# Head outputs turned on VectorE in 32 x 32 squares, layer-norm rows kept on chip, second-norm transposes moved behind later products: one layer of a hybrid conformer / mLSTM backbone

## Chip, core and metric

The kernel runs on one core of one Trainium2 chip. The metric is the device time of one execution, in microseconds (us). TensorE (PE) does matmuls and transposes, VectorE (DVE) and ScalarE (ACT) work element by element, GpSimd (POOL) does small odd work and issues some DMAs, SyncE (SP) issues nearly all other DMAs. Each engine works through its own list of instructions strictly in that list's order; an instruction whose data or buffer isn't ready holds up all that stand behind it on its engine.

## What is computed

One layer (D = 1024) on 512 latent tokens with a prefix of 256 context tokens, all in float32:

```
h  = modulate(rmsnorm(x))                        # six modulation vectors from silu(c) @ w_mod
p  = h @ w_in                                    # GLU, q, k, v, output gate, mLSTM gates, two branch gates
u  = dwconv31(p0 * sigmoid(p1))
A  = silu(layernorm(u)) @ w_conv_out             # conformer branch
hm = rms(bidirectional mLSTM(q, k, v)) * norm_g * sigmoid(p5)    # 4 heads of 512
B  = hm @ w_mlstm_out
x  = x + gate1 * ((sigmoid(gA) * A + sigmoid(gB) * B) @ w_out)
x  = x + gate2 * (relu(modulate(rmsnorm(x)) @ w1) ** 2 @ w2)
out = rmsnorm(x) * final_g
```

## The kernel before

Every float32 product is done as three matmuls of split operands, high x high, high x low, low x high (`mm3`, one line each, L104 to L106). A weight piece of 128 x 1024 (`wpiece`) is loaded by SP into `wraw` (3 buffers), cast to its high part `whi` on ACT (L99), and its low part `wlo` is made on DVE (L100); `whi` and `wlo` have 4 buffers each, so the cast of a piece has to wait until the matmuls of the piece four earlier are over. PSUM is shared out in two rings of four banks, `bank` and `bank_a`.

A planner sets the order of the instructions on every engine when the kernel is built, from the order in which the code is written, its estimates of durations, and a few explicit bounds (`issue_after`). What stands in the list then is fixed.

The stages that the change touches, in order of time:

1. **Head gates** (`finish`, L300): eight transposes make `pz` in PSUM, a copy on DVE (L305) brings it into `zm`. It is used by all heads; the next projection's matmuls (`p`) take over the PSUM bank.
2. **Heads** (`attend`, L448 to L560): for each of 4 heads and 4 token tiles t, the output `po` (128 tokens x 512) is normed into `hm` on ACT and DVE (L553, L555). `store` then transposes `hm` on PE in four blocks of 128 x 128 (`th`, L541), ACT copies them out scaled by the norm weight (L544) into `st`, and SP stores 256 KB to `hd` in DRAM, in runs of 512 B (L546).
3. **Layer norm of the conformer branch** (`lnfinish`, L397): mean and inverse deviation (`lns`) are written to DRAM (`lnd`) and come back as `lnr`. The branch's 8 tiles `cv` (one buffer named "big") are loaded from DRAM, normed on DVE (L665, L666), put through SiLU on ACT (L667) and split into `act` (L109, L110).
4. **Gate pieces and conformer output**: the last four branch-gate products `pab` (i = 12 to 15) each hold one of the four `bank` buffers until ACT has taken their sigmoid (L678, `sig12` to `sig15`). The conformer output products `pc`, with the pieces of `wco`, follow on PE and need `act`, the first `wco` piece, and a free bank, hence `sig12`. `hmload` reads the heads' output back (`hraw`), and splits it into `hmT`, whose space is that of earlier tiles.
5. **Modulation dots** (`mod`, L654): 32 dots of 128 x 1024 on DVE with rows `wmt` that POOL loads, spread between weight pieces; the last eight make the second gate vector, which goes through `row` (a transpose `pr` and a trip through DRAM) to the row `ga2`.
6. **Output product and second norm** (L785 to L816): for each of 4 token tiles, the last part of `pwo`, the residual `x`, two squares with sums (L799), the factor, two scaled halves `xh` (L808, L810), two groups of four transposes `pt` (L813), and the split into `h2T`. The first feed-forward products (`ff1(0)`, `pf`) run over the first 256 tokens, then over the second 256.

Of the kernel before, what the change touches and what calls it, by code (L numbers as in the profile page):

```python
# [47 lines left out]
def block(ctx, tc, a, out):  # L48
# [22 lines left out]
    zm = cst.tile([P, 8, 64], F32, name="zm")  # L71

# [15 lines left out]
    wlast = [None]  # L88

# [13 lines left out]
    def mm3(dst, l, r, start, stop):  # L103
        mm(dst, lhsT=l[0], rhs=r[0], start=start, stop=False)  # L104
        mm(dst, lhsT=l[0], rhs=r[1], start=False, stop=False)  # L105
        mm(dst, lhsT=l[1], rhs=r[0], start=False, stop=stop)  # L106

    def split(hi, lo, src):
        nc.scalar.copy(out=hi, in_=src)  # L109
        nc.vector.tensor_tensor(out=lo, in0=src, in1=hi.bitcast(F32), op=ALU.subtract)  # L110
# [25 lines left out]
    lnd = dr.tile([2, P, T], F32, name="lnd")  # L136
# [8 lines left out]
    with ExitStack() as hs:  # L145
# [108 lines left out]
        def gates():  # L254
            with tc.tile_pool(name="p1", bufs=1) as p1:
# [44 lines left out]
                def finish():  # L300
                    pz = bank("pz")
                    for i in range(8):
                        nc.tensor.transpose(pz[:, i * 64:(i + 1) * 64], Z[:, i // 4, (i % 4) * P:(i % 4 + 1) * P],
                                            ident[0:64, 0:64])
                    nc.vector.tensor_copy(out=zm.rearrange("p a b -> p (a b)"), in_=pz)  # L305
# [74 lines left out]
        ln = {n: hqa.tile([P, T], F32, name=f"ln{n}") for n in ("m0", "s1", "s2")}  # L380
# [16 lines left out]
        def lnfinish():  # L397
            mu, rv = ln["s1"], ln["s2"]
            p1_, p2_ = bank("ps1"), bank("ps2")
            mm(p1_, lhsT=ones, rhs=ln["s1"], start=True, stop=True)  # L400
            mm(p2_, lhsT=ones, rhs=ln["s2"], start=True, stop=True)
            nc.scalar.activation(out=mu, in_=p1_, func=AF.Copy, scale=1.0 / D)
            sq = hq2.tile([P, T], F32, tag="cacc", name="sq")
            nc.scalar.activation(out=sq, in_=mu, func=AF.Square)
            nc.vector.scalar_tensor_tensor(out=rv, in0=p2_, scalar=1.0 / D, in1=sq, op0=ALU.mult, op1=ALU.subtract)
            nc.vector.tensor_scalar(out=rv, in0=rv, scalar1=0.0, scalar2=None, op0=ALU.max)
# [41 lines left out]
        def attend(h, he, he2, khi, klo, qhi, qlo, more, mid):  # L448
# [87 lines left out]
            pend = None  # L536

            def store(t, hm):
                th = bank_a("th")
                for i in range(4):  # L540
                    nc.tensor.transpose(th[:, i * P:(i + 1) * P], hm[:, i * P:(i + 1) * P], ident)  # L541
# [4 lines left out]
                nc.sync.dma_start(out=hd[4 * h:4 * h + 4, :, t * P:(t + 1) * P].rearrange("i p t -> p i t"), in_=st)  # L546
            for t in range(NT):
# [15 lines left out]
            return lambda: store(*pend)  # L563
# [20 lines left out]
        for h in range(H):  # L584
            if h:
                kh = k_proj(h)
                last()
                if h == H - 1:
                    glu_tile(7)
                qh = q_proj(h)  # L590
            if h < H - 1:
                last = attend(h, he, he2, *kh, *qh, lambda: glu_steps(2 * h + 1), None)
            else:
                last = attend(h, he, he2, *kh, *qh,
                              lambda: [lambda i=i: ab_early(i) for i in range(NS + NX, NS + NX + NE)], lnend)
            if h < H - 1:
                glu_tile(2 * h + 2)
        last()


    with ExitStack() as fs:
# [47 lines left out]
        def mod():  # L649
# [3 lines left out]
            with tc.issue_after(wlast[0].ins):  # L653
# [10 lines left out]
        for j in range(KT):  # L664
            nc.vector.tensor_tensor(out=cv[j], in0=cv[j], in1=lnr[0], op=ALU.subtract)  # L665
            nc.vector.tensor_tensor(out=cv[j], in0=cv[j], in1=lnr[1], op=ALU.mult)  # L666
            lsilu = nc.scalar.activation(out=cv[j], in_=cv[j], func=AF.Silu, scale=ccol(O_LG + j), bias=ccol(O_LB + j))  # L667
# [24 lines left out]
        def hmload(k):  # L692
# [7 lines left out]
            split(hm_[k][:, 0, :], hm_[k][:, 1, :], raw)  # L700
# [68 lines left out]
        while mraw:  # L769
            mod()  # L770
# [14 lines left out]
        for t in range(NT):  # L785
            tt = slice(t * P, (t + 1) * P)
            sq = m2p.tile([P, 4], F32, tag="ss", name="ss")
            def last_part(n):
                nn = slice(n * 512, (n + 1) * 512)
                for k in range(NP1, KT):  # L790
                    w = ws[k]
                    mm3(po[2 * t + n], (yT[k][:, 0, tt], yT[k][:, 1, tt]), (w[0][:, 0, nn], w[1][:, 0, nn]),
                        False, k == KT - 1)

            def residual(n):
                nn = slice(n * 512, (n + 1) * 512)
                nc.vector.tensor_tensor(out=x1[t][:, nn], in0=po[2 * t + n], in1=x1[t][:, nn], op=ALU.add)
                xh = t2("xh")
                nc.scalar.activation(out=xh, in_=x1[t][:, nn], func=AF.Square, scale=1.0 / 32.0,  # L799
                                     accum_out=sq[:, n:n + 1])  # L800
            for n in range(2):
                last_part(n)
                residual(n)
            rstd2(sq)
            for hf in range(2):
                hh = slice(hf * 512, (hf + 1) * 512)
                xh = t2("xh")
                nc.vector.scalar_tensor_tensor(out=xh, in0=x1[t][:, hh], scalar=sq[:, 3:4], in1=aff2[:, hh],  # L808
                                               op0=ALU.mult, op1=ALU.mult)
                nc.vector.tensor_tensor(out=xh, in0=xh, in1=sh2[:, hh], op=ALU.add)  # L810
                pt = bank_a("pt2")
                for k in range(4):
                    nc.tensor.transpose(pt[:, k * P:(k + 1) * P], xh[:, k * P:(k + 1) * P], ident)  # L813
# [6 lines left out]
        ga2 = row(modc[:, 5, :], m1p.tile([P, D], F32, tag="r2", name="ga2"))  # L820
# [3 lines left out]
        def w1load(g):  # L824
            r = []
            for i in range(4):
                w = wpiece(a["w1"][4 * g + i], (KT, P))
                r.append([[w[p_][:, k, :] for k in range(KT)] for p_ in range(2)])
            return r

        def ff1(g, ws):
# [4 lines left out]
            for o, n in ((0, 256), (256, 256)) if g == 0 else ():  # L836
                for i in range(4):
# [152 lines left out]
```

## Time and profile before

| what | value |
|---|---|
| median of 3 runs | 1356.4 us (1356.16 to 1357.19) |
| the profiled execution, its own time | 1357.05 us |
| its span, first to last instruction | 1355.3 us |
| busy: PE, DVE, ACT, POOL | 1324.4, 936.7, 602.5, 68.9 us |
| mean granted TensorE clock | 0.995 of full |
| HBM read and written | 163.0 and 12.3 MB, 129 GB/s over the span |

The 1.75 us between the profiled execution's time and its span lie outside the instructions. PE works for 98% of the span, so the time is told by the PE's work and by the few places where it stands idle or runs at a lower clock.

### The profile page before, as it was taken

Reading aid. Unit: us, or ns where it says so; the run is one execution under the profiler, and the core shown is the slowest. Engines: PE = TensorE matmul, PEld = TensorE weight load, DVE = VectorE, ACT = ScalarE, POOL = GpSimd, SP = SyncE. Lnnn points to the kernel's source line nnn. Section 1 sums busy time; section 2 is a strip of 40 time slices with the busy share of each in tenths; the row PEclk is TensorE's granted clock in tenths of the full one; section 3 lists DMA queues with packets and bytes.
Section 4 is the critical chain, followed back from the end, with each engine's and each line's share of the span. In section 5 each row is a group of like instructions: output and inputs, shape, how many; then the busy total and the mean of one; then the engine's idle time right before and its main releaser. Section 6 shows DMA issues by size and latency. Waiting matters only on the chain.

```text
span 1355.3 us, 16676 instructions
## 1 busy us (share of the span) xinstructions
PE 1324.4 (98%) x6266; PEld 1104.1 (81%) x6266; DVE 936.7 (69%) x1457; ACT 602.5 (44%) x912; POOL 68.9 (5%) x231
## 2 busy tenths in 40 slices
PE   5999999999999999999999999999999999999997
PEld 3788788888888888888888878888798888888885
DVE  5789978489674896748995477766684454554535
ACT  4548664346533465344635274322354323342223
POOL 2000100000000000000000000100000000000001
PEclk9999999999999999999999999999989999999999
DMA  9793233223332233322334479765633322333202
GB/s 329 288 334 110 89 112 105 62 63 101 104 94 67 64 100 107 96 63 66 106 96 127 124 249 312 262 189 200 219 106 96 97 92 63 123 109 109 73 22 78
DMA packets 65205, 176.36 MB, mean 130 GB/s; under 512 B 6594, under 2 KB 19042, under 8 KB 65124
## 3 DMA queue, kind: packets, MB, share of 16 engines
q1 hardware_dynamic: 60516, 158.51, 36.0%
q0 software_dynamic: 4608, 16.78, 3.9%
q8 instruction: 49, 0.80, 0.2%
q14 instruction: 32, 0.26, 0.1%
HBM read 162.99 MB, written 12.27 MB: 129 GB/s over the span
## 4 chain that ended last, share of the span: by engine, by line
PE 88%; DVE 4%; ACT 2%; DMA 2%; issue 1%; POOL 1%; SPq 0%; POOLq 0%; ACTq 0%; DVEq 0%
PE pf L104 8%; PE pf L105 8%; PE pf L106 8%; PE pv L105 3%; PE pv L104 3%; PE pv L106 3%; PE pym L106 2%; PE pym L105 2%; PE pym L104 2%; PE p L104 2%; PE p L106 2%; PE p L105 2%; PE pq L106 2%; PE pq L104 2%; PE pq L105 2%; PE pg L104 2%
## 5 line engine op out<-in xcount | busy, mean ns | idle before, releaser
L99 ACT CAST whi<-wraw 128x1024 fp32r<-128x1024 f32 (+1 forms) x159 | 164.9, 1040 | 305.7 <-PE pv L106 74.6
L100 DVE TENSOR_TENSOR wlo<-wraw,whi 128x1024 fp32r<-128x1024 f32 (+1 forms) x159 | 191.6, 1206 | 87.9 <-ACT whi L99 87.4
L372 DVE SCALAR_TENSOR_TENSOR ca<-up,col,ca 128x512 f32<-128x512 f32 x240 | 179.5, 748 | 5.7 <-ACT ca L370 0.9
L332 DVE SCALAR_TENSOR_TENSOR cacc<-craw,col,cacc 128x512 f32<-128x512 f32 (+1 forms) x128 | 110.7, 876 | 0.0
L864 ACT CAST w2h<-w2raw 128x1024 fp32r<-128x1024 f32 x32 | 32.3, 1052 | 156.3 <-PE pf L106 124.8
L105 PE MATMUL pf<-w2l,fT 128*128 128x512 f32 x256 | 99.6, 390 | 0.0
L104 PE MATMUL pf<-w2h,fT 128*128 128x512 f32 x256 | 99.2, 390 | 0.2 <-ACT w2h L864 0.2
L106 PE MATMUL pf<-w2h,fT 128*128 128x512 f32 x256 | 99.5, 389 | 0.0
L884 DVE TENSOR_TENSOR x<-pf,x 128x512 f32<-128x512 f32 x64 | 44.0, 689 | 65.8 <-PE pf L106 65.7
L104 PE MATMUL pf<-h2T,whi 128*128 128x512 f32 x224 | 87.1, 389 | 0.0
L105 PE MATMUL pf<-h2T,whi 128*128 128x512 f32 x224 | 87.1, 389 | 0.0
L106 PE MATMUL pf<-h2T,wlo 128*128 128x512 f32 x224 | 87.1, 389 | 0.0
L104 PE MATMUL pv<-whi,hT 128*128 128x512 f32 x192 | 75.4, 393 | 0.0
L106 PE MATMUL pv<-whi,hT 128*128 128x512 f32 x192 | 74.7, 389 | 0.0
L105 PE MATMUL pv<-wlo,hT 128*128 128x512 f32 x192 | 74.7, 389 | 0.0
L862 DVE TENSOR_TENSOR w2raw<-w2raw,ga 128x1024 f32<-128x1024 f32 x32 | 39.2, 1225 | 47.5 <-DMA w2raw<-in_w 46.4
L104 PEld LDWEIGHTS pf<-w2h,fT 128*128 128x128 f32 x256 | 48.0, 188 | 10.7 <-ACT w2h L864 0.7
L105 PEld LDWEIGHTS pf<-w2l,fT 128*128 128x128 f32 x256 | 48.1, 188 | 10.6 <-DVE w2l L869 0.7
L106 PEld LDWEIGHTS pf<-w2h,fT 128*128 128x128 f32 x256 | 48.1, 188 | 9.8
L104 PE MATMUL p<-whi,hT 128*128 128x512 f32 x128 | 50.8, 397 | 2.2 <-DVE zm L305 2.2
L869 DVE TENSOR_TENSOR w2l<-w2raw,w2h 128x512 fp32r<-128x512 f32 x64 | 40.7, 686 | 15.0 <-ACT w2h L864 15.0
L104 PE MATMUL pg<-hT,whi 128*128 128x512 f32 x128 | 50.6, 395 | 0.0
(354 smaller groups left out, 3344.1 us busy)
## 6 DMA issues: line engine op xcount, KB each, us to landing
wm<-in_wmt SPq DMA_DIRECT2D x32, 512.0 KB, 6.0
wmt<-in_wmt POOLq DMA_DIRECT2D x32, 512.0 KB, 4.7
wraw<-in_wqk SPq DMA_DIRECT2D x32, 512.0 KB, 3.5
wraw<-in_w SPq DMA_DIRECT2D x32, 512.0 KB, 4.7
w2raw<-in_w SPq DMA_DIRECT2D x32, 512.0 KB, 3.6
wraw<-in_wglu SPq DMA_DIRECT2D x16, 512.0 KB, 3.8
wraw<-in_wp SPq DMA_DIRECT2D x16, 512.0 KB, 3.6
wraw<-in_wv SPq DMA_DIRECT2D x16, 512.0 KB, 3.5
```

What stands on the lines that cost most here:

```text
L99: nc.scalar.copy(out=hi[:, s], in_=raw[:, s])
L100: wlast[0] = nc.vector.tensor_tensor(out=lo[:, s], in0=raw[:, s], in1=hi[:, s].bitcast(F32), op=ALU.subtract)
L104: mm(dst, lhsT=l[0], rhs=r[0], start=start, stop=False)
L105: mm(dst, lhsT=l[0], rhs=r[1], start=False, stop=False)
L106: mm(dst, lhsT=l[1], rhs=r[0], start=False, stop=stop)
L332: nc.vector.scalar_tensor_tensor(out=acc[:, :n], in0=raw[:, d:d + n], scalar=ccol(wc + d), in1=acc[:, :n], op0=ALU.mult, op1=ALU.add)
L372: nc.vector.scalar_tensor_tensor(out=accv, in0=up[:, :, d:d + 64], scalar=w_, in1=accv, op0=ALU.mult, op1=ALU.add)
L862: nc.vector.tensor_tensor(out=raw, in0=raw, in1=ga2, op=ALU.mult)
L864: nc.scalar.copy(out=hi, in_=raw)
L869: nc.vector.tensor_tensor(out=l_, in0=raw[:, nn], in1=hi[:, nn].bitcast(F32), op=ALU.subtract)
L884: nc.vector.tensor_tensor(out=x1[t][:, nn], in0=pf, in1=x1[t][:, nn], op=ALU.add)
```

## The change

- The heads' `th` transposes and scaled copies are gone. DVE turns `hm` within 32 x 32 squares (one instruction for 128 x 512), and four DMAs for each token tile put the squares in their places in DRAM, in runs of 128 B. The norm weight is multiplied in when `hmload` splits the rows.
- `store` follows its tile at once, no longer one tile later.
- `lns` stay on chip, without the trip to DRAM.
- `zm` is copied by ACT.
- In the second norm, the squares' unused result goes into the PSUM of `pwo`; the transposes of tile 0 are bound behind the last part of tile 2, those of tile 1 behind that of tile 3, those of tiles 2 and 3 behind the first half of `ff1(0)`.
- The dots that are left over at that point come after the splits into `h2T`, and `ga2` is made after `ff1(0)`.

```diff
+    lns = [cst.tile([P, T], F32, name=f"lns{i}") for i in range(2)]
...
-                    nc.vector.tensor_copy(out=zm.rearrange("p a b -> p (a b)"), in_=pz)
+                    nc.scalar.copy(out=zm.rearrange("p a b -> p (a b)"), in_=pz)
...
-        ln = {n: hqa.tile([P, T], F32, name=f"ln{n}") for n in ("m0", "s1", "s2")}
+        ln = {"m0": hqa.tile([P, T], F32, name="lnm0"), "s1": lns[0], "s2": lns[1]}
...
-            nc.sync.dma_start(out=lnd[0], in_=mu)
-            nc.sync.dma_start(out=lnd[1], in_=rv)
...
-            pend = None
             def store(t, hm):
-                th = bank_a("th")
+                st = he.tile([P, HD], F32, tag="st", name="st")
+                nc.vector.transpose(out=st, in_=hm)
                 for i in range(4):
-                    nc.tensor.transpose(th[:, i * P:(i + 1) * P], hm[:, i * P:(i + 1) * P], ident)
-                st = he.tile([P, 4, P], F32, tag="st", name="st")
-                for i in range(4):
-                    nc.scalar.activation(out=st[:, i, :], in_=th[:, i * P:(i + 1) * P], func=AF.Copy,
-                                         scale=ccol(O_MG + 4 * h + i))
-                nc.sync.dma_start(out=hd[4 * h:4 * h + 4, :, t * P:(t + 1) * P].rearrange("i p t -> p i t"), in_=st)
+                    nc.sync.dma_start(
+                        out=hd[4 * h:4 * h + 4, :, t * P + 32 * i:t * P + 32 * i + 32].rearrange(
+                            "k (b r) c -> r (k b) c", r=32),
+                        in_=st[32 * i:32 * i + 32, :].rearrange("r (b c) -> r b c", c=32))
             for t in range(NT):
...
-                if pend:
-                    store(*pend)
-                pend = (t, hm)
+                store(t, hm)
...
-        lnr = []
-        for i in range(2):
-            r_ = t2(f"lnr{i}")
-            nc.sync.dma_start(out=r_, in_=lnd[i])
-            lnr.append(r_)
...
-        def mod():
+        def mod(after=None):
             if not mraw:
                 return
             ch, j, raw = mraw.popleft()
-            with tc.issue_after(wlast[0].ins):
+            with tc.issue_after((after or wlast[0]).ins):
...
-            split(hm_[k][:, 0, :], hm_[k][:, 1, :], raw)
+            nc.scalar.activation(out=hm_[k][:, 0, :], in_=raw, func=AF.Copy, scale=ccol(O_MG + k))
+            nc.vector.scalar_tensor_tensor(out=hm_[k][:, 1, :], in0=raw, scalar=ccol(O_MG + k),
+                                           in1=hm_[k][:, 0, :].bitcast(F32), op0=ALU.mult, op1=ALU.subtract)
...
-        while mraw:
-            mod()
...
+        sqs = [m2p.tile([P, 4], F32, name=f"ss{t}", bufs=1) for t in range(NT)]
+        xhs = {}
+        tlast = [None]
+        def last_part(t):
             tt = slice(t * P, (t + 1) * P)
-            sq = m2p.tile([P, 4], F32, tag="ss", name="ss")
-            def last_part(n):
+            for n in range(2):
                 nn = slice(n * 512, (n + 1) * 512)
                 for k in range(NP1, KT):
                     w = ws[k]
                     mm3(po[2 * t + n], (yT[k][:, 0, tt], yT[k][:, 1, tt]), (w[0][:, 0, nn], w[1][:, 0, nn]),
                         False, k == KT - 1)
-            def residual(n):
-                nn = slice(n * 512, (n + 1) * 512)
                 nc.vector.tensor_tensor(out=x1[t][:, nn], in0=po[2 * t + n], in1=x1[t][:, nn], op=ALU.add)
-                xh = t2("xh")
-                nc.scalar.activation(out=xh, in_=x1[t][:, nn], func=AF.Square, scale=1.0 / 32.0,
-                                     accum_out=sq[:, n:n + 1])
-            for n in range(2):
-                last_part(n)
-                residual(n)
-            rstd2(sq)
+                nc.scalar.activation(out=po[2 * t + n], in_=x1[t][:, nn], func=AF.Square, scale=1.0 / 32.0,
+                                     accum_out=sqs[t][:, n:n + 1])
+            rstd2(sqs[t])
+            return mlast[0]
+        def scaled(t, hf):
+            hh = slice(hf * 512, (hf + 1) * 512)
+            xh = xhs[t, hf] = t2("xh")
+            nc.vector.scalar_tensor_tensor(out=xh, in0=x1[t][:, hh], scalar=sqs[t][:, 3:4], in1=aff2[:, hh],
+                                           op0=ALU.mult, op1=ALU.mult)
+            nc.vector.tensor_tensor(out=xh, in0=xh, in1=sh2[:, hh], op=ALU.add)
+        def turned(t, after):
+            tt = slice(t * P, (t + 1) * P)
             for hf in range(2):
-                hh = slice(hf * 512, (hf + 1) * 512)
-                xh = t2("xh")
-                nc.vector.scalar_tensor_tensor(out=xh, in0=x1[t][:, hh], scalar=sq[:, 3:4], in1=aff2[:, hh],
-                                               op0=ALU.mult, op1=ALU.mult)
-                nc.vector.tensor_tensor(out=xh, in0=xh, in1=sh2[:, hh], op=ALU.add)
                 pt = bank_a("pt2")
-                for k in range(4):
-                    nc.tensor.transpose(pt[:, k * P:(k + 1) * P], xh[:, k * P:(k + 1) * P], ident)
+                with tc.issue_after(after.ins):
+                    for k in range(4):
+                        nc.tensor.transpose(pt[:, k * P:(k + 1) * P], xhs[t, hf][:, k * P:(k + 1) * P], ident)
                 ptv = pt.rearrange("p (k t) -> p k t", k=4)
                 kk = slice(4 * hf, 4 * hf + 4)
-                split(h2T[:, 0, kk, tt], h2T[:, 1, kk, tt], ptv)
+                tlast[0] = split(h2T[:, 0, kk, tt], h2T[:, 1, kk, tt], ptv)
+        last_part(0)
+        scaled(0, 0)
+        scaled(0, 1)
+        last_part(1)
+        scaled(1, 0)
+        turned(0, last_part(2))
+        scaled(1, 1)
+        l3 = last_part(3)
+        scaled(2, 0)
+        turned(1, l3)
+        def rest(after):
+            scaled(2, 1)
+            scaled(3, 0)
+            turned(2, after)
+            scaled(3, 1)
+            turned(3, after)
...
-        ga2 = row(modc[:, 5, :], m1p.tile([P, D], F32, tag="r2", name="ga2"))
...
+                mod(tlast[0])
...
+                if o:
+                    rest(mlast[0])
...
+            if g == 0:
+                ga2 = row(modc[:, 5, :], m1p.tile([P, D], F32, tag="r2", name="ga2"), m_)
```

How the lists of the engines change at the places that the prediction speaks of (rows of one kind in a row are counted, x4; names of the kernel after have other line numbers).

ACT before, from the last SiLUs of `cv` to the sigmoids `sig12` to `sig15` of the four `pab` (named here by their buffers, 6730 to 6733); the `whi` in it is that of the second `wco` piece, that of the first stands ahead of the first SiLU:

```order
L667 ACTIVATE cv<-cv,col 128x512 x2
L109 CAST act<-cv 128x512 x2
L667 ACTIVATE cv<-cv,col 128x512
L109 CAST act<-cv 128x512 x3
L99 CAST whi<-wraw 128x1024
L678 ACT_TABLE_LOAD
L678 ACTIVATE sig_6730<-pab 128x512
L678 ACTIVATE sig_6731<-pab 128x512
L678 ACTIVATE sig_6732<-pab 128x512
L109 CAST hmT<-hraw 128x512
L678 ACTIVATE sig_6733<-pab 128x512
```

The same place on ACT after, from the first two `wco` pieces on; `sig12` to `sig15` are 6643 to 6646:

```order
L101 CAST whi<-wraw 128x1024 x2
L654 ACT_TABLE_LOAD
L654 ACTIVATE cv<-cv,col 128x512 x4
L101 CAST whi<-wraw 128x1024
L654 ACTIVATE cv<-cv,col 128x512 x3
L101 CAST whi<-wraw 128x1024
L654 ACTIVATE cv<-cv,col 128x512
L111 CAST act<-cv 128x512 x8
L687 ACTIVATE hmT<-hraw,col 128x512 x3
L665 ACT_TABLE_LOAD
L665 ACTIVATE sig_6643<-pab 128x512
L665 ACTIVATE sig_6644<-pab 128x512
```

All four `wco` casts, eight splits and three of `hmT` now stand ahead of `sig12`, where two casts and the eight splits stood before.

DVE after, from the third `wco` piece's low part (first row) and the last `hm` turned to the splits of `act` and `hmT`; `lns_82` and `lns_83` are the rows that stay on chip:

```order
L102 TENSOR_TENSOR wlo<-wraw,whi 128x1024
L538 STREAM_TRANSPOSE st<-hm 128x512
L652 TENSOR_TENSOR cv<-cv,lns_82 128x512 x2
L653 TENSOR_TENSOR cv<-cv,lns_83 128x512 x2
L652 TENSOR_TENSOR cv<-cv,lns_82 128x512
L641 SCALAR_TENSOR_TENSOR wmt,modc<-wmt,cB 128x1024
L653 TENSOR_TENSOR cv<-cv,lns_83 128x512
L102 TENSOR_TENSOR wlo<-wraw,whi 128x1024
L641 SCALAR_TENSOR_TENSOR wmt,modc<-wmt,cB 128x1024
L644 TENSOR_TENSOR modc<-modc,col 128x8
L112 TENSOR_TENSOR act<-cv,act 128x512 x8
L688 SCALAR_TENSOR_TENSOR hmT<-hraw,col,hmT 128x512 x8
```

Before, the whole norm of `cv` and the splits `act` stood ahead of the first `wlo` of `wco`; now the first three `wlo`, three dots and two turned tiles stand ahead of and between the passes of the norm, and the fourth `wlo` with a dot ahead of the splits.

ACT after, at the head gates:

```order
L321 COPY craw<-pk 128x256
L101 CAST whi<-wraw 128x1024
L322 COPY craw<-pl 128x512
L306 COPY zm<-pz 128x512
L331 ACTIVATE cacc<-craw,col 128x770
```

The copy `zm` stands right behind the copy of `pl` and ahead of the next convolution step; before, it was on DVE, behind two steps of convolutions (`ca`, `cacc`).

PE after, the second half of the second norm, at the turn between the two halves of `ff1(0)`:

```order
L108 MATMUL pf<-h2T,w1l 128x256
L805 MATMUL pt_8265<-ident,xh 128x128 x4
L805 MATMUL pt_8272<-ident,xh 128x128 x4
L805 MATMUL pt_8282<-ident,xh 128x128 x4
L106 MATMUL pf<-h2T,w1h 128x256 x4
L805 MATMUL pt_8289<-ident,xh 128x128 x4
```

The groups are those of tiles 2 and 3; before, they stood between matmuls of the last parts and of the first half.

More of the change, by code (lines that the diff above doesn't have):

```diff
@@ L88, in block @@
     wlast = [None]
+    mlast = [None]
     def wpiece(src, shape, scale=None):
@@ L105, in mm3 @@
         mm(dst, lhsT=l[0], rhs=r[1], start=False, stop=False)
-        mm(dst, lhsT=l[1], rhs=r[0], start=False, stop=stop)
+        mlast[0] = mm(dst, lhsT=l[1], rhs=r[0], start=False, stop=stop)
     def split(hi, lo, src):
         nc.scalar.copy(out=hi, in_=src)
-        nc.vector.tensor_tensor(out=lo, in0=src, in1=hi.bitcast(F32), op=ALU.subtract)
+        return nc.vector.tensor_tensor(out=lo, in0=src, in1=hi.bitcast(F32), op=ALU.subtract)
     hT = [hp.tile([P, 2, TOK], F32R, tag="h", name=f"hT{k}") for k in range(KT)]
@@ L135, in block @@
     sd = dr.tile([NS + NX + NE, P, T], F32, name="sd")
-    lnd = dr.tile([2, P, T], F32, name="lnd")
     queue = deque()
@@ L562, in attend @@
             pump(9)
-            return lambda: store(*pend)
         glu_tile(0)
@@ L586, in block @@
                 kh = k_proj(h)
-                last()
                 if h == H - 1:
@@ L591, in block @@
             if h < H - 1:
-                last = attend(h, he, he2, *kh, *qh, lambda: glu_steps(2 * h + 1), None)
+                attend(h, he, he2, *kh, *qh, lambda: glu_steps(2 * h + 1), None)
             else:
-                last = attend(h, he, he2, *kh, *qh,
+                attend(h, he, he2, *kh, *qh,
                               lambda: [lambda i=i: ab_early(i) for i in range(NS + NX, NS + NX + NE)], lnend)
@@ L597, in block @@
                 glu_tile(2 * h + 2)
-        last()
     with ExitStack() as fs:
@@ L664, in block @@
         for j in range(KT):
-            nc.vector.tensor_tensor(out=cv[j], in0=cv[j], in1=lnr[0], op=ALU.subtract)
-            nc.vector.tensor_tensor(out=cv[j], in0=cv[j], in1=lnr[1], op=ALU.mult)
+            nc.vector.tensor_tensor(out=cv[j], in0=cv[j], in1=lns[0], op=ALU.subtract)
+            nc.vector.tensor_tensor(out=cv[j], in0=cv[j], in1=lns[1], op=ALU.mult)
             lsilu = nc.scalar.activation(out=cv[j], in_=cv[j], func=AF.Silu, scale=ccol(O_LG + j), bias=ccol(O_LB + j))
@@ L699, in hmload, with row @@
             nc.sync.dma_start(out=raw, in_=hd[k])
-            split(hm_[k][:, 0, :], hm_[k][:, 1, :], raw)
+            nc.scalar.activation(out=hm_[k][:, 0, :], in_=raw, func=AF.Copy, scale=ccol(O_MG + k))
+            nc.vector.scalar_tensor_tensor(out=hm_[k][:, 1, :], in0=raw, scalar=ccol(O_MG + k),
+                                           in1=hm_[k][:, 0, :].bitcast(F32), op0=ALU.mult, op1=ALU.subtract)
         for k in range(16):
             queue.append(lambda k=k: hmload(k))
-        def row(src, r_):
+        def row(src, r_, after=None):
             pr = bank("pr")
-            nc.tensor.transpose(pr[0:KT, 0:P], src, ident)
+            with tc.issue_after((after or mlast[0]).ins):
+                nc.tensor.transpose(pr[0:KT, 0:P], src, ident)
             t_ = t2("rowt", P)
@@ L784, in block @@
         h2T = big([P, 2, KT, T], F32R, "h2T")
-        for t in range(NT):
+        sqs = [m2p.tile([P, 4], F32, name=f"ss{t}", bufs=1) for t in range(NT)]
+        xhs = {}
+        tlast = [None]
+        def last_part(t):
             tt = slice(t * P, (t + 1) * P)
-            sq = m2p.tile([P, 4], F32, tag="ss", name="ss")
-            def last_part(n):
+            for n in range(2):
                 nn = slice(n * 512, (n + 1) * 512)
@@ L903, in block @@
             ft = ff1(g, w1)
+            m_ = mlast[0]
             if g + 1 < NG:
                 w1 = w1load(g + 1)
+            if g == 0:
+                ga2 = row(modc[:, 5, :], m1p.tile([P, D], F32, tag="r2", name="ga2"), m_)
             if prev is not None:
```

## The prediction

> **What bounds the kernel now.** I read the head of the page first, then the waits of PE, then its busy time by windows.
>
> ```profile
> span 1355.3 us, 16676 instructions
> PE 1324.4 (98%) x6266; PEld 1104.1 (81%) x6266; DVE 936.7 (69%) x1457; ACT 602.5 (44%) x912; POOL 68.9 (5%) x231
> ...
> DMA  9793233223332233322334479765633322333202
> ...
> PE 88%; DVE 4%; ACT 2%; DMA 2%; issue 1%; POOL 1%; SPq 0%; POOLq 0%; ACTq 0%; DVEq 0%
> ```
>
> PE carries the chain; the DMA engines are busy for two or three tenths of most slices. A change gains by taking instructions off PE, or by shortening a stretch in which PE stands or runs slowly, and loses by making a new one. The waits of PE (total, times, longest, us) that the change touches:
>
> ```profile
> PE pt L813 <- DVE xh L810: 2.9, 1, 2.9
> ...
> PE p L104 <- DVE zm L305: 2.2, 1, 2.2
> ...
> PE th L541 <- DVE hm L555: 0.7, 1, 0.7
> ```
>
> Two of them cost more than their length. In the busy time by windows (PE, PEld, DVE, ACT, POOL, then the granted clock) the window after a wait runs at half speed:
>
> ```profile
> 160.49:163.90 3.41, 1.19 (x6) 0.68 (x5) 3.41 (x5) 2.57 (x4) 1.21 (x2) 1.00 0.94 306
> 163.90:167.31 3.41, 3.41 (x10) 2.63 (x9) 3.41 (x5) 3.38 (x5) 2.30 (x3) 0.50 0.02 7
> ...
> 979.69:983.10 3.41, 1.44 (x7) 0.86 (x5) 2.56 (x4) 1.17 (x4) 1.58 (x2) 1.00 0.81 257
> 983.10:986.51 3.41, 2.49 (x10) 2.40 (x11) 3.35 (x6) 1.07 (x3) 0.00 (x0) 0.50 0.27 111
> 986.51:989.92 3.41, 3.41 (x9) 2.64 (x9) 2.30 (x4) 1.44 (x5) 0.86 (x2) 0.50 0.00 0
> 788.55:791.96 3.41, 2.71 (x17) 2.00 (x16) 0.75 (x1) 1.72 (x6) 0.74 (x2) 1.00 0.36 116
> 791.96:795.37 3.41, 3.41 (x17) 2.81 (x16) 0.60 (x1) 1.14 (x4) 0.00 (x0) 1.00 0.92 262
> ```
>
> PE busy for 1.19 or 1.44 us of a window of 3.41 is followed by clock 0.50; busy for 2.71 is not. A half-speed window costs half its busy time, 1.7 us at most. The limit lies between 1.44 and 2.71 us.
>
> The Trainium skill ("TensorE: Matmul & The Clock Gate", Part 1: The HAM clock gate) lets the clock fall after at least one idle window of about 3.4 us. The rows disagree: here a window with 1.19 us of work was enough. By that rule the waits would cost their length alone, and the sum below would be 1.7 us higher; the rows decide.
>
> **Heads.** 64 transposes go, in 16 groups of four.
>
> ```profile
> 788.76 0.60 PE L541 MATMUL th<-ident,hm 128*128 128x128 f32 x4
> 789.11 0.48 PE L104 MATMUL pab<-hT,whi 128*128 128x512 f32 x1
> 789.43 0.40 PE L105 MATMUL pab<-hT,whi 128*128 128x512 f32 x1
> 789.66 0.40 PE L106 MATMUL pab<-hT,wlo 128*128 128x512 f32 x1
> ...
> 781.76 0.43 DVE L406 TENSOR_SCALAR lns<-lns 128x512 f32<-128x512 f32 x1
> ...
> L546 SPq DMA_DIRECT2D hd<-st x16: 359/377/382, 256.6 to 794.4; - x16
> ...
> DMA to landing us min/median/max: 2.3/3.8/6.9
> ```
>
> A group takes 0.35 us of PE from start to start: 16 x 0.35 = 5.6, and the wait of 0.7 goes with it, so **-6.3 us**. All of it is on the path, since PE has no gap around the groups. ACT is freed of the copies. DVE gets 16 turns of 128 x 512; no row shows one. The bounds are a one-source pass of the same size (0.43 us, L406) and a two-source pass of 1024 elements (1.22, the `wlo` below); I take the two-source pass of 512, 0.69 us, as the `zm` row below. That is 11 us on a DVE that is 69% busy, beside PE's products. SP issues 64 stores for 16, 48 x 0.38 = 18 us more, spread over four heads and ahead of weight loads that were issued long before their use. The norm weight's multiply makes 16 passes of DVE slightly longer, off the path. `lns` kept on chip takes four DMAs out of SP's list and nothing off PE.
>
> **Gate copy.**
>
> ```profile
> 161.57 1.02 DVE L332 SCALAR_TENSOR_TENSOR cacc<-craw,col,cacc 128x770 f32<-128x770 f32 x1
> 162.50 0.69 DVE L305 COPY zm<-pz 128x512 f32<-128x512 f32 x1
> ...
> 160.90 0.58 ACT L321 COPY craw<-pl 128x512 f32<-128x512 f32 x1
> ```
>
> On ACT the copy stands right behind the copy of `pl`, which ends at 161.48; with the same 0.58 us it ends at about 162.1, against 163.2. The wait shrinks by 1.1 to about 1.2 us. PE's busy time in that window rises to 1.19 + 1.1 = 2.3, above 1.44 and below 2.71; nearer the upper one, so I take the half-speed window as gone: 1.7. Together **-2.8 us** (bounds -1.1 and -2.8). Behind the copy on ACT stands a convolution step, late by 0.6, which PE doesn't await.
>
> **Gate pieces to conformer output.** Here the new ACT list costs. The rows before:
>
> ```profile
> 796.05 1.06 ACT L99 CAST whi<-wraw 128x1024 fp32r<-128x1024 f32 x1 [1.69 <-PE pab L105]
> ...
> 798.42 2.23 ACT L667 ACTIVATE cv<-cv,col 128x512 f32<-128x512 f32 x3
> ...
> 802.49 1.13 ACT L109 CAST act<-cv 128x512 fp32r<-128x512 f32 x2
> ...
> 808.24 1.05 ACT L99 CAST whi<-wraw 128x1024 fp32r<-128x1024 f32 x1
> 809.31 1.28 ACT L678 ACT_TABLE_LOAD   x1
> 810.61 1.58 ACT L678 ACTIVATE sig<-pab 128x512 f32<-128x512 f32 x3
> 812.05 0.63 ACT L109 CAST hmT<-hraw 128x512 fp32r<-128x512 f32 x1
> ...
> 794.77 0.69 DVE L665 TENSOR_TENSOR cv<-cv,lnr 128x512 f32<-128x512 f32 x1 [3.37 <-DMA cv<-cdr]
> ...
> 805.44 4.29 DVE L110 TENSOR_TENSOR act<-cv,act 128x512 fp32r<-128x512 f32 x7
> 809.66 1.22 DVE L100 TENSOR_TENSOR wlo<-wraw,whi 128x1024 fp32r<-128x1024 f32 x1
> 810.79 1.22 DVE L654 SCALAR_TENSOR_TENSOR wmt<-wmt,cB 128x1024 f32<-128x1024 f32 x1
> ```
>
> The first row shows the first `wco` cast wait for the end of the first of the last four gate pieces (`pab12`, 796.05), whose `whi` buffer it takes. Each piece is 24 matmuls of 0.227 us from start to start (789.43 and 789.66 above), 5.45 us, so `pab15` ends 16.3 later, at 812.4; call that moment F. `sig12` is done at 811.1, before F: no wait of PE today.
>
> After, the casts of all four `wco` pieces stand ahead of `sig12`; the fourth takes the buffer of `pab15` and can't start before F. Behind it on ACT: one SiLU (0.72), eight `act` casts (0.52 each from start to start), three `hmT` (0.6), the table load and `sig12`. That alone is 1.05 + 0.72 + 4.2 + 1.6 + 1.28 + 0.6 = 9.4 us in which `pc` has no bank. This is the lower bound. DVE makes it longer: its list has four `wlo` (1.15), dots (1.2) and turned tiles between the steps of the norm of `cv`. The first `wlo` waits for a cast at F - 16.3 + 1.1, so the norm starts at about F - 12.1 (F - 17.6 today: 794.8). Then nine passes of 0.6 (F - 6.7), `wlo`, a pass, a dot (F - 3.7), `wlo`, a turn (F - 1.9), five passes (F + 1.1), a dot, a pass (F + 2.9), the fourth `wlo` and a dot (F + 5.3), eight splits `act` (4.8: F + 10.1). `hmT` takes the space of `cv` and waits for the last split; three of them, the table and `sig12` bring it to F + 13.6. I take 13.7, and 1.7 for the half-speed restart: **+15.4 us** (bounds 9.4 and 17).
>
> **Second norm.**
>
> ```profile
> 985.17 0.59 ACT L109 CAST h2T<-pt 128x512 fp32r<-128x512 f32 x1 [4.28 <-PE pt L813]
> ...
> 981.94 1.41 DVE L808 SCALAR_TENSOR_TENSOR xh<-x,ss,aff 128x512 f32<-128x512 f32 x2 [0.85 <-POOL ss L82]
> 983.27 1.28 DVE L810 TENSOR_TENSOR xh<-xh,sh 128x512 f32<-128x512 f32 x2
> ...
> 999.47 0.25 ACT L708 COPY rowt<-pr 8x128 f32<-8x128 f32 x1
> ...
> 1007.52 2.59 DVE L862 TENSOR_TENSOR w2raw<-w2raw,ga 128x1024 f32<-128x1024 f32 x2 [0.93 <-DMA ga<-rowd]
> ```
>
> Today this stretch loses the wait of 2.9 and half of 2.49 + 3.41 us at half speed, 2.95: 5.9 in all. After, tile 0's transposes have the last part of tile 2 as cover (18 matmuls, 4.1 us) and don't wait. What is late next: tile 1's come right ahead of the first `pf`, which need their casts. On ACT these stand behind two squares of tile 3, and those behind tile 3's residuals and tile 2's scaling on DVE: two casts of 0.59 and these put the first `pf` about 3.2 us after the transposes, and the low part (0.69, behind a `wlo`) another 0.6. At the turn to the second half, tiles 2 and 3 take DVE's scaled halves, casts and splits in a row, with four matmuls as cover: about 1.9 us. 5.7 in all, and 0.7 for the clock, as each idle stretch may or may not fall into one window: **+0.5 us** (bounds -5.9, all covered, and +3.2, two slow windows). The last dots and `ga2` lie beside `ff1(0)` and group 1's products; `ga2` takes 8 us from its copy out of PSUM to DVE's first use (999.47 to 1007.52), and the first product with its weights comes after group 1's 96 matmuls, 21.8 us after `ff1(0)`; so I cost it at nothing. Should the last dots' rows land late, `pr` would hold PE, by no more than the 2 us that fit under the upper bound.
>
> **Sum.** -6.3 - 2.8 + 15.4 + 0.5 = +6.8 on the profiled execution's 1357.05: 1363.9. That execution stood 0.65 above the median, so 1363.2.
>
> **Rivals.**
> - *The gate pieces don't stall* (A). If `sig12` still came before F, through casts that don't wait for `pab15`, 1356.4 - 6.3 - 2.8 + 0.5 = 1347.8, faster. For it: the same place shows no wait today. Against it: the first row above, where such a cast waited. It decides at F: each us of `sig12` behind F costs one, and from 8.6 on the gain is spent. Chance 0.15.
> - *ACT's list alone sets the stall, and the second norm gains* (B): 9.4 + 1.7 there, and 3 gained at the second norm, if only its first idle stretch is left: 1356.4 - 6.3 - 2.8 + 11.1 - 3 = 1355.4. For it: DVE's idle rows; against it: its passes are all needed for `act`. Chance 0.17.
> - *The stores in 128 B runs are slow* (C). One store lands in 2.3 to 6.9 us; four times the runs at one price for each would make 9.2 from the shortest, over the 4.1 us between tiles. `st` has one buffer, so DVE's next turn would wait, in the last head ahead of the norm of `cv`: some 5 us more on the stall, 1368. For it: ACT once waited 2.5 us for `st`; against it: DMA queues idle for most of a head. Chance 0.10.
>
> The Trainium skill ("DMA: Bandwidth & Descriptors", Specifications) puts line rate at 512 B or more for one transfer and has smaller ones read, modify and write. No run here shows it; by it rival C is the likelier.
>
> **How the numbers follow.** The forecast as summed has 0.58. About 0.2% (2.7 us) is what a measurement of this kernel can tell from no change. Slower: the forecast and C less 0.04, 0.64. Same: half of B and that rest, 0.12. Faster: A and the other half of B, 0.24. The range from 1351 to 1369 takes in B, C and the forecast's bounds (9.4 and 17 at the stall, either sign at the second norm); A is left out.
>
> **What would show it.** Right: no `th`, `p` waiting for ACT's `zm` for about 1.2 us and clock 1.00 in the window after; `pc` waiting 9 to 15 us for ACT's `sig12`, with DVE's `act` splits after F; `pf` waiting twice for `h2T`. Wrong: `pc` starting within 2 us of F, a wait of PE on `wlo` or `hmT` in the heads, `st` waited for by DVE, or `pf` waiting for `ga2`'s row.

## The result and the profile after

The changed kernel takes 1365.15 us (median of 4 runs, 1364.16 to 1367.77) against 1356.8 (median of 4, 1356.16 to 1357.94): 1.0064 times the time before, 95% interval 1.0046 to 1.0081. The prediction was 1363.2 us, slower.

The head of the page, for the profiled execution of 1364.73 us:

```profile
span 1363.0 us, 16541 instructions
PE 1317.5 (97%) x6202; PEld 1098.6 (81%) x6202; DVE 947.1 (69%) x1472; ACT 586.7 (43%) x848; POOL 71.7 (5%) x231
...
q1 hardware_dynamic: 85284, 157.47, 36.3%
...
PE 85%; DVE 7%; ACT 3%; issue 2%; DMA 2%; POOL 1%; SPq 0%; POOLq 0%; DVEq 0%; ACTq 0%
```

PE has 64 instructions less and 6.9 us less to do, and the span is 7.7 us longer. The part of the chain on DVE went from 4% to 7%. Where PE waits now (total, times, longest, us):

```profile
PE pc L106 <- ACT sig L665: 13.7, 1, 13.7
...
PE pf L106 <- ACT h2T L111: 4.3, 2, 3.5
...
PE p L106 <- ACT zm L306: 1.0, 1, 1.0
...
PE spc L107 <- DVE klo L112: 0.6, 1, 0.6
PE pt L805 <- DVE xh L796: 0.3, 1, 0.3
```

The waits on `th` and, but for 0.3 us, on `xh` are gone, that on `zm` is halved; new are `pc`, `pf` and `klo`. ACT and DVE around the end of `pab15` (F, 802.2 us) show how the first comes about:

```profile
785.83 1.05 ACT L101 CAST whi<-wraw 128x1024 fp32r<-128x1024 f32 x1 [4.48 <-PE pab L107]
791.27 1.06 ACT L101 CAST whi<-wraw 128x1024 fp32r<-128x1024 f32 x1 [4.38 <-PE pab L107]
...
803.17 1.03 ACT L101 CAST whi<-wraw 128x1024 fp32r<-128x1024 f32 x1
804.70 0.81 ACT L654 ACTIVATE cv<-cv,col 128x512 f32<-128x512 f32 x1 [0.50 <-DVE cv L653]
805.42 4.24 ACT L111 CAST act<-cv 128x512 fp32r<-128x512 f32 x8
812.13 1.95 ACT L687 ACTIVATE hmT<-hraw,col 128x512 fp32r<-128x512 f32 x3 [2.47 <-DVE act L112]
814.09 1.28 ACT L665 ACT_TABLE_LOAD   x1
815.38 2.06 ACT L665 ACTIVATE sig<-pab 128x512 f32<-128x512 f32 x4
...
786.91 1.23 DVE L102 TENSOR_TENSOR wlo<-wraw,whi 128x1024 fp32r<-128x1024 f32 x1 [3.87 <-ACT whi L101]
788.06 1.22 DVE L641 SCALAR_TENSOR_TENSOR wmt<-wmt,cB 128x1024 f32<-128x1024 f32 x1
...
789.83 1.25 DVE L652 TENSOR_TENSOR cv<-cv,lns 128x512 f32<-128x512 f32 x2
...
807.19 4.91 DVE L112 TENSOR_TENSOR act<-cv,act 128x512 fp32r<-128x512 f32 x8
```

The first cast idles 4.48 us for the end of `pab12`; its `wlo` holds DVE, so the norm of `cv` starts at 789.8, F - 12.4. The `act` splits end at 812.0, F + 9.9; three `hmT` and a table load follow, and `sig12` to `sig15` stand last. The windows after it and those of the second norm (PE, PEld, DVE, ACT, POOL, clock):

```profile
816.08:819.50 3.42, 3.42 (x8) 2.74 (x9) 0.00 (x0) 1.38 (x4) 0.00 (x0) 0.50 1.07 391
...
993.58:996.99 3.41, 0.62 (x6) 0.38 (x4) 3.38 (x7) 2.21 (x5) 0.06 (x1) 1.00 0.02 5
996.99:1000.40 3.41, 2.71 (x11) 2.48 (x12) 3.41 (x6) 2.07 (x5) 1.67 (x2) 0.50 0.25 59
1000.40:1003.82 3.42, 3.42 (x18) 3.42 (x18) 3.13 (x4) 0.00 (x0) 0.00 (x0) 0.50 0.51 146
```

I compared the start of the first matmul of a kind on PE in every trace with that in the trace before. The steps say where time went, in us (minus is a gain):

| stretch | after | e1 | e2 | e3 | e4 | e5 | e6 | e7 | e8 |
|---|---|---|---|---|---|---|---|---|---|
| start to first `pg` (62.75 before) | +0.3 | +2.0 | +3.0 | -1.0 | +2.1 | +2.1 | +0.1 | +2.6 | +1.5 |
| to the first `spc` (gate copy) | -3.0 | -0.1 | -2.8 | -3.4 | -3.8 | -3.9 | -2.7 | -0.7 | -3.2 |
| to F (heads) | -7.5 | -8.8 | -7.5 | -7.5 | -7.8 | -7.7 | -7.7 | -8.8 | -7.5 |
| F to the first `pc` | +13.9 | +13.8 | +6.2 | 0.0 | +13.9 | 0.0 | 0.0 | 0.0 | +1.1 |
| to the first `pwo` (`pc`, `pym`) | +1.7 | +2.4 | +2.1 | +9.2 | +1.7 | +1.6 | +4.7 | +1.8 | +3.1 |
| to the end of `ff1(0)` (second norm) | +2.1 | -1.1 | +2.6 | +2.2 | -1.3 | -2.7 | -2.4 | -1.8 | -2.6 |
| to the end | +0.1 | -0.1 | +0.3 | +0.3 | +0.3 | 0.0 | +0.2 | +0.2 | +0.2 |
| span against 1355.3 | +7.7 | +8.2 | +4.0 | -0.2 | +5.1 | -10.6 | -7.8 | -6.6 | -7.5 |

The first row isn't the change's: it differs by up to 4.0 us (e3 and e2) between kernels that are the same up to there. Each column is one execution, in e1 and e2 the slowest of its kernel (2.1 and 3.5 us above the median), in e5 the fastest (2.9 below); medians even this out better.

### The profile page after: what moved, and what is told of

It is laid out like the page before. It is cut to its first block, busy times and chain, and to the rows that moved or that the text cites. A ratio compares the mean times of both kernels' runs of the same rounds, so it can differ in the third digit from the quotient of the medians.

```text
span 1363.0 us, 16541 instructions
## 1 busy us (share of the span) xinstructions
PE 1317.5 (97%) x6202; PEld 1098.6 (81%) x6202; DVE 947.1 (69%) x1472; ACT 586.7 (43%) x848; POOL 71.7 (5%) x231
## 4 chain that ended last, share of the span: by engine, by line
PE 85%; DVE 7%; ACT 3%; issue 2%; DMA 2%; POOL 1%; SPq 0%; POOLq 0%; DVEq 0%; ACTq 0%
PE pf L106 8%; PE pf L107 8%; PE pf L108 8%; PE pv L108 3%; PE pv L107 3%; PE pv L106 3%; PE pg L106 2%; PE pg L108 2%; PE pym L106 2%; PE pym L107 2%; PE pg L107 2%; PE pym L108 2%; PE pq L108 2%; PE pq L107 2%; PE pq L106 2%
```

## Experiments

The edits are shown shortened, with `...` where lines are left out; remarks behind `#` are not in the kernels.

**e1: the heads' turn alone, on the kernel before.** `store` and `hmload` as in the diff of the change; `zm`, `lns` and the second norm as before.

```diff
-                th = bank_a("th")
...
+                nc.vector.transpose(out=st, in_=hm)
...
-                pend = (t, hm)
+                store(t, hm)
```

> The kernel before with the heads' turn on VectorE alone (with the norm weight moved along). My theory: the removed transposes and their waits give about 8.9 us, as the two traces show between the first head and pab15; and the ACT list already has three wco casts and three hmT ahead of sig12, so that pc stalls 10 to 12 us and restarts at half speed (1.7): 1356.6 - 8.9 + 12.7 = about 1360, 1358 to 1362. Rival: the stall comes from the rows kept on chip, through which the norm of cv is planned earlier; then the turn alone shows the gain and no stall of over 2 us at pc: about 1348.

1363.16 us, 1.0053 times before (1.0040 to 1.0065), 1.2 us above the range given. The heads gain 8.8 us and `pc` stalls as in the whole change:

```profile
PE pc L104 <- DMA sig<-sd: 13.7, 1, 13.7
```

The DMA named here isn't what PE waits for: in e3 `pc` starts at 800.5 us while these loads are still issued up to 808.8, and here it starts at 819.3, 0.1 us after ACT's `sig12`:

```profile
818.60 2.07 ACT L671 ACTIVATE sig<-pab 128x512 f32<-128x512 f32 x4
```

So it is the bank of `sig12`, as in the kernel after, where the wait is of the same length. The 10 to 12 us that I gave it were too few. The rival falls: the rows kept on chip aren't needed for the stall. The turn with what comes with it (no copies out of PSUM on ACT, no one-tile delay of `store`, the scaling in `hmload`) is enough for the planner to write casts of `wco` and `hmT` ahead of `sig12`; which of the three does it was not separated.

**e2: ACT's list bound, on the kernel after.**

```diff
+        with tc.issue_after(ca) if ca is not None else ExitStack():     # wpiece: the cast goes behind ca
+            nc.scalar.copy(out=hi[:, s], in_=raw[:, s])
...
+            with tc.issue_after(sigi[3].ins):       # sig15, in hmload
+                nc.scalar.activation(out=hm_[k][:, 0, :], in_=raw, func=AF.Copy, scale=ccol(O_MG + k))
...
+            w = wpiece(a["wco"][j], (KT, P), ca=sigi[2].ins if j else None, da=None)    # sig14
```

> The kernel after with ACT's list bound: wco casts from the second piece on behind sig14, hmT behind sig15; VectorE's passes follow where the planner then puts them. My theory: the 13.7 us at pc come from what stands ahead of sig12 on ACT; with it gone sig12 follows the last act cast, about 5 us behind the end of pab15: stall about 5 and a window at half speed, 1365.2 - 9 = about 1356, 1353 to 1358. Rival: the late start of the norm of cv on VectorE (first wlo, late loads) sets it, and ACT's order doesn't matter: stall still over 10 us, 1362 or more.

1357.59 us, 1.0007 (0.9998 to 1.0016), in the range given. The stall falls from 13.9 to 6.2 us, and the rival, with over 10 us left, falls with it. What is left has its start on DVE, behind the first `wlo`, and its end in ACT's row of splits:

```profile
794.69 1.28 ACT L656 ACT_TABLE_LOAD   x1 [4.87 <-DVE cv L655]
...
805.09 4.25 ACT L113 CAST act<-cv 128x512 fp32r<-128x512 f32 x8 [0.84 <-DMA hd<-st]
809.36 1.28 ACT L667 ACT_TABLE_LOAD   x1
810.66 2.06 ACT L667 ACTIVATE sig<-pab 128x512 f32<-128x512 f32 x4
```

**e3: both lists bound.** `sig12` to `sig14` right behind the last SiLU, the `act` splits behind them; the first two `wlo` of `wco` behind the norm of `cv`, the others behind the splits; the four dots of this stage moved to the later `pc`.

```diff
-        for i in range(NS + NX + NE, 16):
+        for i in range(NS + NX + NE, 15):           # 12 to 14; ab_tile(15) follows the act splits
             ab_tile(i)
-            mod()
...
+            with tc.issue_after(sigi[2].ins):       # sig14
+                alast = split(aj[:, 0, :], aj[:, 1, :], cv[j])
...
+            w = wpiece(a["wco"][j], (KT, P), ca=sigi[2].ins if j > 1 else None, da=lcv.ins if j < 2 else alast.ins)
...
+            if j > 3:
+                mod()
```

(`ca` and `da` are what `wpiece` puts its cast and its low part behind; `lcv` is the last pass of the norm of `cv`.)

> The kernel after with both lists bound: sig12 to sig14 right behind the last SiLU, the act casts and the third and fourth wco casts behind them, hmT behind sig15; on VectorE the first two wlo behind the norm of cv, dots behind these. My theory: with nothing of the later stage ahead, the norm starts at once when cv has landed and pc starts within 1.5 us of the end of pab15, no half-speed window: 1365.2 - 14.5 = about 1350.5, 1349 to 1353. Rival: the loads of cv, which can't start before the heads' buffers are free, set the stall; then 4 us or more stay at pc: 1354 or more.

1358.94 us, 1.0016 (1.0006 to 1.0025), where I had given 1349 to 1353: the number was wrong and the place right. `pc` starts at F without a gap, so neither the loads of `cv` nor anything else of the stage needs more time than the products give. The time is lost behind it:

```profile
PE pc L110 <- DVE wlo L104: 4.6, 2, 3.6
...
PE pym L110 <- DVE wlo L104: 1.7, 1, 1.7
```

```profile
816.80 0.75 DVE L693 SCALAR_TENSOR_TENSOR hmT<-hraw,col,hmT 128x512 fp32r<-128x512 f32 x1 [5.75 <-ACT hmT L692]
818.70 1.41 DVE L693 SCALAR_TENSOR_TENSOR hmT<-hraw,col,hmT 128x512 fp32r<-128x512 f32 x2 [1.14 <-ACT hmT L692]
820.03 1.22 DVE L104 TENSOR_TENSOR wlo<-wraw,whi 128x1024 fp32r<-128x1024 f32 x1
...
816.04 0.72 ACT L692 ACTIVATE hmT<-hraw,col 128x512 fp32r<-128x512 f32 x1 [7.12 <-DMA hraw<-hd]
```

With a window at half speed behind them (821.66 to 825.07, 1.7 us) these waits make 8.0 of the 9.2 us in the table. A `wlo` that PE needs stands behind `hmT` splits that PE needs only 30 us later, and these wait for rows (`hraw`) that SP issues behind twelve `sig` loads. It is the same fault as the one I had removed, one stage on.

**e4: the kernel after with the second norm, the leftover dots and `ga2` as before.**

```diff
-        last_part(0)
-        scaled(0, 0)
...
+        for t in range(NT):                         # last parts, residuals, norm, transposes of t
...
+        while mraw:
+            mod()
```

> The kernel after with the second norm, the leftover dots and ga2 as they were before. By the traces the moved second norm loses 2.15 us (from +5.4 to +7.55 between the first pwo and the end of ff1(0)), so this comes out at 1363.0, 1362 to 1364. Rival: what is lost there is only the other side of the later start, and the moved transposes gain the 2.9 us of wait they remove: then this is slower than the kernel after, 1367 or more.

1362.17 us, 1.0041 (1.0029 to 1.0054); the kernel after has 1.0064 (1.0046 to 1.0081). The time lies in the range given, but the intervals overlap; the traces separate the two better. The stretch gives -1.3 us here and costs 2.1 with the moved transposes. As the old order alone differs from -2.7 to 0 from trace to trace (the last section says more), the size is open between 2.1 and 4.8 us; its sign isn't, since three traces with the moved transposes (after, e2, e3) stand at +2.1 to +2.6. The rival falls.

**e5: both lists bound, repaired, second norm as before.** As e3, with the loads and splits of `hmT` spread later (one for each of the first three `pc`) and bound behind the last `wlo` made, and the four dots in the `pym` stage.

```diff
-            pump(2)
+            pump((1, 1, 1, 3, 3, 3, 2, 2)[j])
...
+            with tc.issue_after(wlast[0].ins):      # hmload, VectorE's part
```

> The kernel after with ACT's and VectorE's lists bound at the gate pieces, the later hmT bound behind the wco piece that was last made, four dots moved into the next stage, and the second norm as before the change. My theory: heads -8.8, gate copy -2.9 less 1.3 given back at klo, no stall at pc, and the waits on wlo of the run before (6.9 and 2.0 us) gone with hmT no longer ahead of wlo on VectorE: 1356.6 - 10.4 = about 1346, 1344.5 to 1349. Rival: the heads' rows read back (hraw) come late because SP issues them behind twelve sig loads, so that hmT and with it a wlo or pym still waits: 1350 or more.

1349.36 us, 0.9959 (0.9945 to 0.9972), span 1344.7. No stall at `pc`, and of the waits on `wlo` 0.3 us are left:

```profile
PE pt L810 <- DVE xh L807: 2.5, 2, 2.3
...
PE pym L108 <- DVE sig L715: 0.6, 1, 0.6
PE spc L109 <- DVE klo L114: 0.6, 1, 0.6
PE p L108 <- ACT zm L308: 0.4, 1, 0.4
PE pc L110 <- DVE wlo L104: 0.3, 1, 0.3
```

The median lies 0.4 us above the range I gave; the profiled execution (1346.49) lies in its middle. Against the kernel after, the medians are 15.8 us apart. Three edits stand together here (loads, bound, dots), and what each gave was not separated.

**e6: the same with the moved second norm, tile 1's transposes bound behind the first half of tile 3's last part.**

```diff
-        l3 = last_part(3)
+        last_part(3, lambda m: turned(1, m))        # called after the first half
         scaled(2, 0)
-        turned(1, l3)
```

> The same, with the second norm of the kernel after, and tile 1's transposes bound behind the first half of tile 3's last part instead of its end. My theory: the wait of 3.5 us ahead of the first pf comes from tile 1's casts, which stand behind tile 3's squares on ACT and right ahead of their use; with half a last part as cover (2 us) and the casts ahead of the squares about 2.5 of it go, and the norm is level with or 1 to 2 us better than before: 1344 to 1348, no slower than the run without the moved norm by over 1 us. Rival: the low parts on VectorE (residuals and scaling ahead of them) set it, and the wait stays at 3 us or more: 2 us slower than that run.

1349.06 us, 0.9953 (0.9941 to 0.9966), 1.1 us above the range given, but level with e5, so faster than both given kernels as well. The wait ahead of the first `pf` is gone, and 1.8 us now fall between the two groups of transposes of tile 1:

```profile
PE pt L815 <- DVE xh L806: 2.2, 2, 1.8
PE pc L110 <- DVE wlo L104: 1.9, 2, 1.2
PE pym L108 <- DVE sig L716: 1.7, 1, 1.7
...
PE pf L108 <- ACT h2T L113: 0.8, 1, 0.8
```

The stretch stands at -2.4 us, against +2.1 in the kernel after. ACT makes the two casts of tile 1 at 981.24 and 983.24 here, ahead of the last squares of tile 3 (983.73, 987.19), and at 997.07 in the kernel after, behind its squares (994.45, 996.44). So the casts' place was the cause, as the theory said. It is no better than the old order in e5 (-2.7). The waits on `wlo` and `sig`, in the stage before, are longer than in e5 (0.3 and 0.6) and make most of the 3.1 us by which that row of the table is worse; in the code of this stage the two kernels differ only in a bound on the transpose `pr`, and why PE waits longer is not shown.

**e7: e5 with the gate copy back on DVE.**

```diff
-                    nc.scalar.copy(out=zm.rearrange("p a b -> p (a b)"), in_=pz)
+                    nc.vector.tensor_copy(out=zm.rearrange("p a b -> p (a b)"), in_=pz)
```

> The run without the moved norm (e5), with the gate copy back on VectorE. By the traces the copy on ACT gives 2.7 to 3.9 us up to the first spc and 1.3 of it is lost again where PE waits for klo; so this is 1.5 to 2.5 us slower than e5: 1350.5 to 1352, PE waiting 2.2 us for zm, none for klo. Rival: klo's wait has nothing to do with the copy, and the whole 2.9 or more come back: 1352.5 or more; or the half-speed window isn't the copy's: under 1 us.

1350.7 us, 0.9953 (0.9939 to 0.9968): in the range given, but as a ratio to the kernel before the times don't tell it from e5 (0.9959). In the traces the stretch to the first `spc` gains 0.7 instead of 3.9 us, and the heads 8.8 instead of 7.7: by these two traces the copy on ACT is worth about 3.2 - 1.1 = 2.1 us. The window at half speed behind the wait is back (from 166.01 us, as from 163.90 in the kernel before and 165.47 in e1); none of the seven traces with the copy on ACT has it. PE waits here for `zm` and no longer for `klo`:

```profile
PE p L108 <- DVE zm L308: 1.9, 1, 1.9
```

No trace with the copy on DVE waits for `klo`, and all with it on ACT do: `klo` is what comes late next when the copy is early.

**e8: e5 with every store of the heads made twice**, the second time to a place that nothing reads.

```diff
+                for i in (0, 1, 2, 3):
+                    nc.sync.dma_start(out=hd2[...], in_=st[32 * i:32 * i + 32, :]...)
                 for i in range(4):
```

> The run without the moved norm (e5), with every store of the heads made twice, the second time to a place in DRAM that nothing reads: 128 stores for 64, twice the packets of 128 B. My theory: SP and the DMA engines have the room, so PE's waits in the heads stay as they are, and only in the last head, where the loads of cv stand behind stores on SP, 0 to 3 us are added at pc: span within 3 us of e5's 1344.7. Rival (C of the prediction): the small packets are near the limit; turns on VectorE then wait for st, weights come late, PE waits for wlo in the heads: 5 us or more.

One execution of 1349.54 us, span 1347.8 against 1344.7, just over the 3 us that I allowed; with the first row of the table taken out, 3.6 us more. The stretch through the heads is the same to 0.2 us. DVE's turns wait for `st` twice, 2.6 us in all, and most of the cost comes where I had put it, at `pc` and behind it (+1.1 and +1.5):

```profile
L541 DVE STREAM_TRANSPOSE st<-hm x16: 700/708/712, 252.7 to 793.6; 128x512 f32<-128x512 f32 x16
its engine sat idle before it (us, times) until:
  DMA hd<-st: 2.6, 2
```

Even twice the small packets are hidden in the heads, and the 5 us or more of the rival don't show.

## Why the prediction was right

The result lies 2 us above the forecast, on the forecast's side and inside its range, and the stall that decides the sign came by the mechanism forecast. That the sum came so close is in part luck: the heads gained 2.5 us more than forecast (e1), while `klo` and the second norm, 1.3 and 1.6 us, took more than that back. Step by step, from the table and the rows above:

- **Heads**: -6.3 forecast. With `zm` out of the way (e1) the stretch gave -8.8. The term was too small because I counted from the first transpose to the next product, 0.35 us; that product is followed by its second only after 0.32 us (789.11 to 789.43 in the rows of the prediction) instead of 0.23, and with the products behind it a group costs 0.46 us: 16 x 0.46 = 7.4, and the wait 0.9 with its edges. That makes 8.3; the other 0.5 isn't explained. The turn on DVE, which no row had shown, takes 0.704 us; I had taken 0.69. The row of the kernel after:

```profile
L538 DVE STREAM_TRANSPOSE st<-hm x16: 655/704/714, 251.7 to 799.2; 128x512 f32<-128x512 f32 x16
...
DMA to landing us min/median/max: 1.8/2.4/4.2
```

- **Gate copy**: -2.8 forecast, -3.0 measured to the first `spc`, with a wait of 1.0 (1.2 forecast) and no slow window behind the one with 2.40 us of PE work (2.3 forecast):

```profile
160.83:164.24 3.41, 2.40 (x11) 1.75 (x10) 3.41 (x5) 3.38 (x6) 1.82 (x2) 1.00 0.81 287
164.24:167.65 3.41, 3.41 (x17) 2.81 (x16) 3.41 (x5) 3.19 (x5) 2.62 (x3) 1.00 0.59 161
```

Missed was `klo`, which comes out of the convolution steps. It is ready about when it was before (its second part starts on DVE at 175.50 us, before at 175.93), and PE, now 3 us earlier, runs into it: 0.6 us of wait, 1.3 in the heads' stretch (-7.5 against -8.8 in e1). I had counted that chain as one that PE doesn't await. The copy gave 3.0 - 1.3 = 1.7 us net.
- **Gate pieces**: 13.7 of stall and 1.7 of clock forecast, 13.9 and 1.7 measured. The row of events held as worked out: norm of `cv` from F - 12.4 (forecast F - 12.1), last `act` split at F + 9.9 (F + 10.1), `sig12` at F + 13.8 (F + 13.6). e2 and e3 show the cause: the lists. Binding ACT's takes 7.7 us off the stall, binding DVE's as well the other 6.2.
- **Second norm**: +0.5 forecast, +2.1 measured. The idle stretches fell where forecast, and were a little shorter (3.5 and 0.8 us in the wait rows, and 0.3 at the transposes after, against 3.8 and 1.9); the clock was mis-sized: not 0.7, but two windows at 0.50 (996.99 to 1003.82, above), up to 3.1 us, where the old order had lost 2.95.
- **Rivals**: A fell, its place shows the longest wait of all. B fell, since DVE did lengthen ACT's 9.4 us and the second norm lost. C fell: in the kernel after none of the 16 turns waits for `st` (the row above has no wait below it), and the stores land in 1.8 to 4.2 us. Its price of 9.2 us was read from a row that mixes the stores with the later loads of `hraw` (2.3 to 6.9 us); the stores alone landed in 2.3 to 3.7 us before, and the turns come 8 to 11 us apart, not 4.1. By the Trainium skill ("DMA: Bandwidth & Descriptors", Specifications) transfers under 512 B lose line rate. The queue's rows fit and give the size: e1, with the same 158.51 MB as before, has 25,344 packets more and a share of 36.6% of the span instead of 36.0%, and a packet of 128 B took 12.8 ns on average (32,768 of them) where one of 512 B before took 28.3: 1.8 times the time per byte, and still little beside the span.
- **A sum that was short**: the prediction puts its sum 1.7 us higher for the case that waits cost their length alone. The clock terms of the second norm (2.95 before, 0.7 after) would go as well then, so it would be 4.0 higher, about 1367.

## What to carry to other kernels

When work is taken off one engine, read the new lists of the engines around it: a planner that finds ACT free may put casts ahead of the one operation that frees a PSUM bank, and an in-order engine then turns a buffer that isn't free into a stall of the engine that mattered. Bind the operation that PE waits for ahead of work that is needed later, on both engines of the chain, and then look at the next stage for the same fault; here bounds on both engines, a later `pump` and moved dots, with the second norm in its old order or with one group of transposes bound earlier, turned +0.6% into -0.4%. A wait that is removed shows at once what was hidden under it (`zm`, then `klo`).

## What the runs showed of the hardware

The price of a wait depends on where it falls among the clock's windows. In each trace the changes of the clock lie whole multiples of 3.413 us apart, so one of them gives the windows of the whole trace: in the kernel before 163.90 and 983.10 are 240 apart, in e5 60.18 and 1340.18 are 375. The second norm in its old order waits 2.9 us in the kernel before, with 6.8 us at half speed behind it (983.10 and 986.51 in the prediction's rows), and 2.3 us in e5, with none:

```profile
971.54:974.95 3.41, 1.69 (x8) 1.08 (x6) 2.56 (x4) 0.80 (x3) 1.58 (x2) 1.00 0.84 285
974.95:978.37 3.42, 2.88 (x16) 2.39 (x17) 3.42 (x6) 2.14 (x5) 0.27 (x1) 1.00 0.16 63
```

An edge of a window cuts the wait in both; in e5, 1.69 us of work in the worse window kept the clock, where 1.44 us had lost it before. That narrows the prediction's limit, 1.44 to 2.71 us, to about 1.6 in this stage, and it isn't sharp: 1.60 us lost the clock in e1 (991.49 to 994.91), 1.57 kept it in e6 (979.78 to 983.19). Over the five traces with the old order (e1, e4, e5, e7, e8) the same code differs by up to 2.7 us from the kernel before.

The profile's busy time doesn't always tell. At the start, where the kernels are alike, a window of e5 with 3.08 us is followed by half speed, and e5 is 2.1 us later there:

```profile
56.77:60.18 3.41, 3.08 (x9) 1.43 (x10) 1.74 (x2) 3.39 (x6) 0.00 (x0) 1.00 0.07 28
60.18:63.59 3.41, 3.41 (x9) 2.61 (x9) 3.41 (x9) 2.57 (x4) 0.00 (x0) 0.50 0.10 37
```

Of these 3.08 us, 2.06 are four products `pcr` with a single row of weights (56.59 to 58.65), all in this window. In the kernel before an edge at 58.08 falls near the end of the same four (56.14 to 58.20), and the clock stays at 1.00. That such products count for less fits, but no run tests it. The kernel before differs from execution to execution too: a mean clock of 0.997 at 1354.02 us, 0.994 at 1358.33. The Trainium skill ("TensorE: Matmul & The Clock Gate", Part 1: The HAM clock gate) says that the window runs freely and doesn't restart with the kernel, which fits; that a whole idle window of about 3.4 us must come before the clock falls is not what these rows show.
